# A decoder layer's state space tables padded on GpSimd, and its first h made in three steps

## The chip, the cores and the metric

The kernel runs on one NeuronCore of a Trainium2 chip. The metric is the device time of one launch in microseconds (us), taken as the median of several runs. TensorE is called PE in the views of the profile, its weight loads PEld, VectorE DVE, ScalarE ACT, GpSimd POOL, and SP is the engine whose queue issues the DMAs.

## The reference

One layer of a decoder over 256 tokens of width 2048, in float32:

```
mod = silu(c) @ w_ada + b_ada                      # six rows of 2048: sh1, sc1, g1, sh2, sc2, g2
h = rms_norm(x, norm1_g) * (1 + sc1) + sh1
q, k, v, u = split(h @ w_in)                       # 2048 -> 4 x 1024
attn = dilated_attention(rms_norm(q), rms_norm(k), v)   # 8 heads
y = gelu(s5_mixer(u))                              # 64 groups of 16 channels, 64 complex states each
ssm = y * sigmoid(y @ w_glu + b_glu)
x = x + g1 * (concat(rms_norm(attn), rms_norm(ssm)) @ w_out)
h2 = rms_norm(x, norm2_g) * (1 + sc2) + sh2
out = x + g2 * (square(relu(h2 @ w_ff1)) @ w_ff2)
```

The s5_mixer is a linear recurrence with a diagonal complex transition a per group: the state takes a times itself plus B u, and y = Re(C state) + D u.

## The kernel before

**Products.** Every large product is made from a high and a low part: a value v is written as hi, which is v rounded to the type that PE multiplies in one pass (fp32r), and lo = v - hi. Of the four products three are made (line 191, mm3). `split` (line 172) makes the parts of a tile: ScalarE copies v into hi with the rounding, VectorE subtracts. The same is done to each weight piece of 512 KB as it arrives in the ring `raw` of nine buffers (load_w, line 181); its parts are called wh and wl, with three buffers each.

**First h.** x lies transposed in the tile XT, 16 chunks of 128 channels by 256 tokens. rbc is the reciprocal root mean square per token, broadcast over partitions; g1c is (1 + sc1) * norm1_g per channel. make_h(kg) makes four chunks of h in the tiles HA or HB, both parts. Each chunk goes through a VectorE multiplication with rbc in place, a ScalarE pass in place that scales by g1c and adds the shift (line 316), a ScalarE copy that rounds to the high part, and a VectorE subtraction. make_h is called four times, with weight blocks of w_in between the calls.

**Modulation.** The product with w_ada (100 MB) is cut into 96 pieces. Eight of 24 blocks go through PE (line 249, then 260), the others through VectorE, which multiplies a piece of 128x1024 with c and sums it up (line 158). `pump` puts pieces between the other work in program order.

**State space tables.** B times powers of a is built by VectorE in b_step (tiles WB2, WB3), C times powers of a in ca_step (tile CA). Two groups share the 128 partitions, 64 each, and PE needs them block diagonal. So tables full of zeros are laid out by GpSimd memsets, and pad_write copies the lower 64 partitions into one set of columns and the upper 64 into another: two copies of 64 partitions. It fills padB (tile PD, four copies of 512 elements), the two padC (tiles WB0 and WB1, filled twice by toep_half, eight copies of 256 and eight of 768 elements), and wpad (tile PD, filled by four calls of wb_block, eight copies of 256 elements in each). toep_half's products give the tile TO (ScalarE evicts them in 32-partition pieces); wb_block's 16 transposes per call (line 504) give the final WB tiles, which are used much later, when u is complete. All of these copies are made on ScalarE (line 161, through the helper copy).

**Order.** The program is written once in order; a scheduler that simulates it by a model of the engines then decides the order of the instructions of each engine, and puts in the semaphores. Each engine works its own list in order. `issue_after` puts the cbc multiplications and the b_steps behind the end of the first make_h. Behind the first block of w_in come toep_half(0), a second block, toep_half(1), further blocks, make_h(1), and the wb_blocks.

Of the kernel before, what the change touches and what calls it, by code (L numbers as in the profile page):

```python
# [9 lines left out]
F32 = mybir.dt.float32  # L10
F32R = mybir.dt.float32r
I32 = mybir.dt.int32
AF = mybir.ActivationFunctionType
ALU = mybir.AluOpType
# [102 lines left out]
class _K:  # L117
# [5 lines left out]
    def t(self, tag, shape, dt=F32, bufs=1):  # L123
        self.n += 1
        return self.sb.tile(list(shape), dt, name=f"{tag}_{self.n}", tag=tag, bufs=bufs)
# [12 lines left out]
    def mul(self, out, a, b, eng=None):  # L138
        return self.tt(out, a, b, ALU.mult, eng)
# [14 lines left out]
    def stt(self, out, a, s, b, op0, op1, accum=None):  # L154
        if accum is None:
            self.nc.vector.scalar_tensor_tensor(out, a, s, b, op0=op0, op1=op1)  # L156
        else:
            self.nc.vector.scalar_tensor_tensor(out, a, s, b, op0=op0, op1=op1, accum_out=accum)  # L158

    def copy(self, out, a, scale=1.0):  # L160
        self.nc.scalar.activation(out, a, AF.Copy, scale=scale)  # L161

# [35 lines left out]
def _body(nc, tc, I, out, sb, ps):  # L198
    k = _K(nc, tc, I, out, (sb, ps))
    t, tr = k.t, k.tr  # L200
    mul, add, sub, ts, stt, copy = k.mul, k.add, k.sub, k.ts, k.stt, k.copy
# [5 lines left out]
    xTf = t("XT", [P, 16, SEQ])  # L207
# [20 lines left out]
    mod = t("mod", [P, 96])  # L228
# [12 lines left out]
    def ada_pieces(b):  # L241
        c4 = slice(4 * b, 4 * b + 4)
        if b in PE_BLOCKS:
            acc = tr()
            for g in range(4):
# [8 lines left out]
                if g < 3:  # L254
                    yield
            rows = t("rows", [P, NB], bufs=2)
            copy(rows, acc)
            pc = tr()
            for j in range(4):
# [34 lines left out]
    for j in range(16):  # L294
        sq = t("rows", [P, NB], bufs=2)[:, 0:SEQ]
        nc.scalar.activation(sq, xTf[:, j], AF.Square)
        q = 32 * (j % 4)
        mm(pss[q : q + 32, 0:SEQ], onek, sq, start=j < 4, stop=j >= 12)
    copy(rw[:, 1], pss[:, 0:SEQ])
    mm(psb[:, 0:SEQ], sel, rw[:, 1], start=True, stop=True)  # L300
    rbc = t("rbc", [P, SEQ])
# [3 lines left out]
    g1c = t("g1c", [P, 16])  # L305

    hs = {}

    def make_h(kg):
        hs[kg] = t("HA" if kg % 2 == 0 else "HB", [P, 2, 4, SEQ], F32R)  # L310
        c4 = slice(4 * kg, 4 * kg + 4)
        stt(g1c[:, c4], mod[:, 16 + 4 * kg : 20 + 4 * kg], 1.0, col["n1g"][:, c4], ALU.add, ALU.mult)
        for kc in range(4 * kg, 4 * kg + 4):
            v = xTf[:, kc]
            mul(v, v, rbc)
            nc.scalar.activation(v, v, AF.Identity, bias=mod[:, kc : kc + 1], scale=g1c[:, kc : kc + 1])
            end = k.split(hs[kg][:, 0, kc % 4], hs[kg][:, 1, kc % 4], v)
        return end.ins

    accs = {}  # L320
# [11 lines left out]
    def w_in_evict(pp, n):  # L332
        c = "uqkv"[n // 2]
        fresh = (c, n % 2) not in accs
        accs[c, n % 2] = True
        if c not in accs:
            if c in "uv":
                accs[c] = t(c.upper(), [P, 2, AW])
            else:
                if "qk" not in accs:  # L340
                    accs["qk"] = t("QK", [P, 2, 2, AW])
                accs[c] = accs["qk"][:, "qk".index(c)]
        for m in range(2):
            d = accs[c][:, m, NB * (n % 2) : NB * (n % 2) + NB]
            if fresh:
                copy(d, pp[m])
            else:
                add(d, pp[m], d)
# [120 lines left out]
    def pad_write(dst, src):  # L469
        for gp in range(2):  # L470
            pr = slice(64 * gp, 64 * gp + 64)
            copy(dst(gp)[pr], src[pr])


    padB = t("PD", [P, 32, 2, 2, 16])
# [16 lines left out]
    def wb_block(i):  # L492
        if i == 0:
            s5["wpad"] = t("PD", [P, 8, 2, 4, 2, 16])
            nc.gpsimd.memset(s5["wpad"], 0.0)
        wpad, w, rr = s5["wpad"], i // 2, slice(8 * (i % 2), 8 * (i % 2) + 8)
        for b in range(4):
            pad_write(lambda gp: wpad[:, :, :, b, gp, :], by_r(bpow[w][:, 3 - SUB[b], :, rr]))
        wb.append(t(f"WB{i}", [P, 8, 2, P]))
        for r in range(0, 8, 2):  # L500
            pt = tr()
            for e in range(4):
                src = wpad[:, r + e // 2, e % 2].rearrange("p s g j -> p (s g j)")
                nc.tensor.transpose(pt[:, P * e : P * e + P], src, ident)
            copy(wb[i][:, r : r + 2].rearrange("p r i n -> p (r i n)"), pt)
# [9 lines left out]
    def toep_half(h):  # L515
        for i, padC in enumerate(padCs):
            r8 = 16 * h + 8 * i
            pad_write(lambda gp: padC[:, :, :, gp, 0, :], by_r(c0[:, :, r8 : r8 + 8]))
            pad_write(
                lambda gp: padC[:, :, :, gp, 1:, :].rearrange("p r i d j -> p (r i) (d j)"),  # L520
                ca[:, r8 : r8 + 8, :, 0:3, :].rearrange("p r i d j -> p (r i) (d j)"),
            )
        pt = tr()
        pv = pt.rearrange("p (i g d j) -> p i g d j", i=4, g=2, d=4)
        for i in range(4):
            for ri in range(2):
                for q in range(4):
                    r = 4 * i + q
                    mm(
                        pv[32 * q : 32 * q + 32, i], padB[:, 16 * h + r, ri].rearrange("p g j -> p (g j)"),  # L530
                        padCs[r // 8][:, r % 8, ri].rearrange("p g d j -> p (g d j)"),
                        start=i == 0 and ri == 0, stop=False,
                    )
        mm(
            pv[:, :, :, 0, :], ident, dskip[:, 4 * h : 4 * h + 4].rearrange("p r (g j) -> p r g j", g=2),
            start=False, stop=True,
        )
        pq = pt.rearrange("p (i g d) -> p i g d", i=4, g=2)
        for q in range(4):
            for b in range(4):  # L540
                o = 16 * SUB[b]
                tq = toep[32 * b : 32 * b + 32, 16 * h + q : 16 * h + q + 13 : 4].rearrange("p r g s j -> p r g (s j)")
                copy(tq[:, :, :, o:], pq[32 * q : 32 * q + 32, :, :, 0 : 64 - o])
# [47 lines left out]
    s5_small()  # L591
    pump(8)
    h_end = make_h(0)
    ring["tags"] = RINGS[0]
    with tc.issue_after(rbc_end):
# [20 lines left out]
    for n in (6, 7):  # L616
        run(w_in_block(n, [0]), 1)
    make_h(1)
    ring["tags"] = RINGS[1]
    cw = t("T0", [P, 2, 2, 16, 16])  # L620
# [10 lines left out]
    ring["tags"] = RINGS[2]  # L631
    run(w_in_pair(4, [0, 1]), 3)
    make_h(2)
    run(w_in_block(0, [1, 2]), 4)
    run(w_in_block(1, [1, 2]), 4)
# [29 lines left out]
    for j in range(2):  # L665
        for m in range(2):
            v = qk[:, j, m].rearrange("p (h e) -> p h e", h=NH)
# [337 lines left out]
```

## Time and profile before

| | us |
|---|---|
| median of 3 runs | 1260.02 (1258.0 to 1260.76) |
| profiled execution, own time | 1261.61 |
| its span | 1259.8 |
| mean granted PE clock | 0.96 of full |

The span is the time from the first to the last recorded instruction. Busy time is summed by engine; an engine can be busy for a small share of the span and still hold up the others in one stretch, so the rows below are mostly taken by stretches. An idle time is shown with what ended it.

### The profile page before, as it was taken

The page shows a single profiled execution, that of the slowest core. Times are in us where ns is not written, and L with a number is a line of the kernel's source. Part 1 is how long each engine was busy: PE and PEld are TensorE (multiplying, and loading weights), DVE is VectorE, ACT ScalarE, POOL GpSimd, SP SyncE. Part 2 cuts the span into 40 slices and gives each one's busy share as a digit, 9 for nine tenths or more (in the row PEclk, how much of TensorE's full clock was granted, in tenths as well). Part 3 has the DMA queues.
Part 4 walks back from the last instruction along what each step waited for, and adds up shares of the span by engine and source line. Part 5 has one row for each costly group of instructions (what it writes and reads, how often), then busy time and mean ns, then how long its engine had stood idle before and what let it go on. Part 6 is the DMA issues. An engine that isn't in the chain of part 4 may idle for free.

```text
span 1259.8 us, 17899 instructions
## 1 busy us (share of the span) xinstructions
PE 1182.8 (94%) x6818; PEld 985.8 (78%) x6818; DVE 920.6 (73%) x1520; ACT 579.2 (46%) x808; POOL 13.0 (1%) x12
## 2 busy tenths in 40 slices
PE   5779999999988879399999999999999999999998
PEld 1457677866787768388888888888888888888887
DVE  9898679999687998867664567655667666768654
ACT  3789534333475334335444444443344443344432
POOL 3000000000000000000000000000000000000000
PEclk9689999999797989699999999999999999999999
DMA  9898999799574878656666666656667666777760
GB/s 365 308 313 298 357 333 325 259 320 335 212 239 131 289 235 278 232 183 213 219 187 186 212 233 226 214 186 193 221 221 252 190 189 186 236 237 236 227 209 26
DMA packets 82165, 299.58 MB, mean 238 GB/s; under 512 B 9120, under 2 KB 11424, under 8 KB 80288
## 3 DMA queue, kind: packets, MB, share of 16 engines
q1 hardware_dynamic: 82080, 298.45, 70.7%
q8 instruction: 53, 0.87, 0.3%
q14 instruction: 32, 0.26, 0.1%
HBM read 296.31 MB, written 2.10 MB: 237 GB/s over the span
## 4 chain that ended last, share of the span: by engine, by line
PE 76%; DVE 10%; DMA 7%; ACT 5%; issue 2%; DVEq 0%; ACTq 0%
PE acc L848 37%; PE acc L850 19%; DMA raw<-w_ada 6%; PE acc L193 3%; PE acc L194 3%; PE acc L195 3%; DVE wl L136 3%; DVE raw L158 2%; PE tr L249 2%; PE tr L848 1%; PE tr L553 1%; ACT wh L161 1%; ACT WB L161 1%; PE acc L690 1%; DVE XT L156 1%
## 5 line engine op out<-in xcount | busy, mean ns | idle before, releaser
L136 DVE TENSOR_TENSOR wl<-raw,wh 128x1024 fp32r<-128x1024 f32 x360 | 439.8, 1222 | 254.3 <-ACT wh L161 252.0
L161 ACT ACTIVATE wh<-raw 128x1024 fp32r<-128x1024 f32 x360 | 380.9, 1059 | 491.7 <-PE acc L848 336.6
L848 PE MATMUL acc<-CA,wh 128*128 128x512 f32 x608 | 167.8, 397 | 3.6 <-DVE rs L136 3.6
L158 DVE SCALAR_TENSOR_TENSOR raw<-raw,cbc 128x1024 f32<-128x1024 f32 x112 | 136.3, 1220 | 37.7 <-DMA raw<-w_ada 37.0
L848 PE MATMUL acc<-TO,wh 128*128 128x512 f32 x480 | 132.7, 398 | 1.6 <-DVE rows L136 1.6
L848 PEld LDWEIGHTS acc<-CA,wh 128*128 128x128 f32 x608 | 104.1, 188 | 17.7 <-issue 4.1
L848 PE MATMUL acc<-QK,wh 128*128 128x512 f32 x384 | 106.9, 399 | 7.0 <-DVE QK L136 6.9
L850 PEld LDWEIGHTS acc<-CA,wl 128*128 128x128 f32 x608 | 92.4, 188 | 13.5 <-DVE wl L136 0.3
L850 PE MATMUL acc<-CA,wl 128*128 128x256 f32 x608 | 96.2, 281 | 0.0
L848 PEld LDWEIGHTS acc<-TO,wh 128*128 128x128 f32 x480 | 83.0, 189 | 13.0 <-issue 1.8
L850 PEld LDWEIGHTS acc<-TO,wl 128*128 128x128 f32 x480 | 73.2, 188 | 10.6
L848 PEld LDWEIGHTS acc<-QK,wh 128*128 128x128 f32 x384 | 66.4, 190 | 15.9 <-issue 7.4
L850 PE MATMUL acc<-TO,wl 128*128 128x256 f32 x480 | 76.0, 280 | 0.0
L848 PE MATMUL acc<-WB,wh 128*128 128x512 f32 x256 | 69.8, 394 | 0.0
L850 PEld LDWEIGHTS acc<-QK,wl 128*128 128x128 f32 x384 | 58.5, 188 | 7.9
L850 PE MATMUL acc<-QK,wl 128*128 128x256 f32 x384 | 60.3, 279 | 0.0
L193 PE MATMUL acc<-wh,HA 128*128 128x512 f32 x128 | 47.8, 406 | 5.0 <-ACT wh L161 5.0
L194 PE MATMUL acc<-wl,HA 128*128 128x512 f32 x128 | 51.7, 404 | 0.0
L195 PE MATMUL acc<-wh,HA 128*128 128x512 f32 x128 | 50.5, 399 | 0.0
L194 PE MATMUL acc<-wl,HB 128*128 128x512 f32 x128 | 50.2, 396 | 0.2 <-DVE wl L136 0.2
L195 PE MATMUL acc<-wh,HB 128*128 128x512 f32 x128 | 49.2, 395 | 0.0
L193 PE MATMUL acc<-wh,HB 128*128 128x512 f32 x128 | 48.0, 399 | 0.5 <-DVE V L136 0.4
(269 smaller groups left out, 1739.1 us busy)
## 6 DMA issues: line engine op xcount, KB each, us to landing
raw<-w_ff SPq DMA_DIRECT2D x256, 512.0 KB, 4.4
raw<-w_ada SPq DMA_DIRECT2D x158, 512.0 KB, 5.3
raw<-w_in SPq DMA_DIRECT2D x64, 512.0 KB, 6.5
raw<-w_out SPq DMA_DIRECT2D x32, 512.0 KB, 4.9
U<-w_ada SPq DMA_DIRECT2D x8, 1024.0 KB, 7.6
XT<-xT SPq DMA_DIRECT2D x8, 512.0 KB, 5.8
T<-w_ada SPq DMA_DIRECT2D x8, 512.0 KB, 6.6
raw<-w_glu SPq DMA_DIRECT2D x8, 512.0 KB, 8.0
```

The costliest lines, as they stand in the source:

```text
L136: return (eng or self.nc.vector).tensor_tensor(out, a, b, op=op)
L156: self.nc.vector.scalar_tensor_tensor(out, a, s, b, op0=op0, op1=op1)
L158: self.nc.vector.scalar_tensor_tensor(out, a, s, b, op0=op0, op1=op1, accum_out=accum)
L161: self.nc.scalar.activation(out, a, AF.Copy, scale=scale)
L193: mm(ps, xh, wh, start=start, stop=False)
L194: mm(ps, xh, wl, start=False, stop=False)
L195: mm(ps, xl, wh, start=False, stop=stop)
L249: mm(acc[32 * q : 32 * q + 32, :], cpad[:, 4 * g + q, :], raw[:, i, :], start=g == 0, stop=g == 3,)
L553: mm(pv[:, r - r2, ri], wb[r // 8][:, r % 8, ri], u2[:, :, r, :], start=True, stop=True)
L690: mm(pv[pr, r - r8], ca[pr, r, ri].rearrange("p s j -> p (s j)"), H[pr, ri, r, :], start=False, stop=ri == 1,)
L848: mm(pp[e], hi[:, e, kk], xs[kk].rearrange("p s n -> p (s n)"), start=first and kk == 0, stop=False)
L850: mm(pp[e][:, 0:SEQ], lo[:, e, kk], xs[kk][:, 0], start=False, stop=last and kk == 3)
```

## The change

pad_write copies on GpSimd in place of ScalarE. make_h takes three steps for each chunk in place of four: VectorE multiplies x by g1c and by rbc in one instruction, ScalarE adds the shift and writes the rounded high part in one pass, and VectorE adds the shift again and subtracts the high part for the low part. The helper stt_i is stt with the instruction returned.

```
+    def stt_i(self, out, a, s, b, op0, op1):
+        return self.nc.vector.scalar_tensor_tensor(out, a, s, b, op0=op0, op1=op1)
...
         for kc in range(4 * kg, 4 * kg + 4):
-            v = xTf[:, kc]
-            mul(v, v, rbc)
-            nc.scalar.activation(v, v, AF.Identity, bias=mod[:, kc : kc + 1], scale=g1c[:, kc : kc + 1])
-            end = k.split(hs[kg][:, 0, kc % 4], hs[kg][:, 1, kc % 4], v)
+            v, hi, lo, sh = xTf[:, kc], hs[kg][:, 0, kc % 4], hs[kg][:, 1, kc % 4], mod[:, kc : kc + 1]
+            stt(v, v, g1c[:, kc : kc + 1], rbc, ALU.mult, ALU.mult)
+            nc.scalar.activation(hi, v, AF.Identity, bias=sh)
+            end = k.stt_i(lo, v, sh, hi.bitcast(F32), ALU.add, ALU.subtract)
         return end.ins
...
         for gp in range(2):
             pr = slice(64 * gp, 64 * gp + 64)
-            copy(dst(gp)[pr], src[pr])
+            nc.gpsimd.tensor_copy(dst(gp)[pr], src[pr])
```

## Rows read from the trace of the kernel before

**Rows 1.** Page: busy us of each engine, share of the span, instructions.

```profile
PE 1182.8 (94%) x6818; PEld 985.8 (78%) x6818; DVE 920.6 (73%) x1520; ACT 579.2 (46%) x808; POOL 13.0 (1%) x12
```

**Rows 2.** Busy time by stretch; last three: granted PE clock, DMA share, GB/s.

```profile
28.00:56.00 28.00, 18.11 (x132) 9.06 (x133) 22.78 (x43) 17.69 (x29) 0.00 (x0) 0.63 0.88 325
56.00:72.00 16.00, 12.23 (x53) 7.16 (x52) 13.43 (x25) 15.61 (x31) 0.00 (x0) 0.98 0.83 286
72.00:90.00 18.00, 17.39 (x122) 13.70 (x120) 18.00 (x34) 12.39 (x25) 1.82 (x1) 0.83 0.93 320
90.00:126.00 36.00, 31.19 (x161) 24.56 (x162) 31.82 (x60) 35.01 (x69) 0.00 (x0) 1.00 0.90 304
126.00:220.00 94.00, 93.56 (x411) 70.90 (x410) 71.55 (x102) 42.89 (x54) 0.22 (x1) 1.00 0.92 338
```

**Rows 3.** Waits in 26:56, 56:82 and 82:126: total us, times, longest.

```profile
DVE HA L136 <- ACT HA L161: 5.0, 2, 3.5
...
PE acc L193 <- ACT wh L161: 3.8, 1, 3.8
...
PE tr L504 <- ACT PD L161: 4.0, 4, 1.5
...
DVE wl L136 <- ACT wh L161: 4.2, 4, 1.4
```

**Rows 4.** Timeline of VectorE, ScalarE and PE, 28 to 90: start, us, instruction.

```profile
28.16 1.43 DVE L136 TENSOR_TENSOR XT<-XT,rbc 128x256 f32<-128x256 f32 x4
...
47.89 3.42 ACT L161 ACTIVATE WB<-CA 64x768 f32<-64x768 f32 x4 [4.44 <-DVE CA L136]
48.91 0.15 DVE L136 TENSOR_TENSOR mod<-tr,small 128x4 f32<-128x4 f32 x1
51.33 2.07 ACT L316 ACTIVATE XT<-XT,mod,g1c 128x256 f32<-128x256 f32 x4
...
55.48 0.48 PE L193 MATMUL acc<-wh,HA 128*128 128x512 f32 x1
...
70.13 1.06 ACT L161 ACTIVATE wh<-raw 128x1024 fp32r<-128x1024 f32 x1
```

**Rows 5.** ScalarE by form, 25 to 127: busy us, mean ns | idle before.

```profile
L161 ACT ACTIVATE PD<-WB 64x256 f32<-64x256 f32 x32 | 13.3, 417 | 0.7
L161 ACT ACTIVATE WB<-CA 64x768 f32<-64x768 f32 x8 | 6.7, 843 | 4.6 <-DVE CA L136 4.4
L161 ACT ACTIVATE WB<-T 64x256 f32<-64x256 f32 x8 | 3.3, 411 | 5.8 <-DVE T L150 5.8
L161 ACT ACTIVATE PD<-WB 64x512 f32<-64x512 f32 x4 | 2.5, 629 | 4.8 <-DVE WB L136 4.8
L161 ACT ACTIVATE HA<-XT 128x256 fp32r<-128x256 f32 x4 | 1.5, 406 | 0.0
```

**Rows 6.** VectorE and ScalarE by form, whole span, as in rows 5.

```profile
L136 DVE TENSOR_TENSOR XT<-XT,rbc 128x256 f32<-128x256 f32 x16 | 5.6, 419 | 0.0
L156 DVE SCALAR_TENSOR_TENSOR V<-XT,g2c,rbc 128x256 f32<-128x256 f32 x8 | 3.3, 481 | 0.0
L136 DVE TENSOR_TENSOR wl<-raw,wh 128x1024 fp32r<-128x1024 f32 x360 | 439.8, 1222 | 254.3 <-ACT wh L161 252.0
L907 ACT ACTIVATE TO<-V,mod 128x256 fp32r<-128x256 f32 x8 | 3.3, 495 | 3.3 <-DVE V L156 3.3
```

**Rows 7.** Timeline of GpSimd and VectorE, at the start and near 81 us.

```profile
2.47 3.58 POOL L480 MEMSET WB<- 128x2048 f32 x2
4.34 1.74 DVE L152 TENSOR_SCALAR HA<-HA 128x32 f32<-128x32 f32 x1
14.77 0.17 DVE L152 TENSOR_SCALAR HA<-HA 128x32 f32<-128x32 f32 x1
...
80.76 1.82 POOL L495 MEMSET PD<- 128x2048 f32 x1 [69.17 <-PE tr L529]
81.30 0.15 DVE L136 TENSOR_TENSOR adap<-adap 128x1 f32<-128x1 f32 x1
```

## The prediction

> **What bounds the kernel now.** I began with the busy shares of the page: TensorE (PE) is busy 94% of the span, ScalarE (ACT) 46% [rows 1]. Over the whole kernel ScalarE bounds nothing, so a relief of ScalarE can only count in a stretch where its queue is the last to deliver. The second view was therefore the busy time by stretch [rows 2]. The reader is to see three things there. From 28 to 126 us PE is idle for 28 - 18.11, 16 - 12.23, 18 - 17.39 and 36 - 31.19, together 19.1 us; from 126 to 220 us it is idle for 0.4 us in 94. ScalarE is busy 15.61 of 16 us and 35.01 of 36 us in two of those stretches, and 42.89 of 94 behind them. And VectorE (DVE) is nearly full in the same stretches: its idle time there is 5.2 + 2.6 + 0 + 4.2 = 12.0 us. All that the diff edits, but for the later uses of make_h, runs before 126 us. So the question is how far PE's full stretch can start before 126 us; what it gains there should reach the end, since PE stays full behind it.
>
> The third view was the waits [rows 3]: PE waits 3.8 us at one place for the high part of a weight tile (wh) from ScalarE, 4.0 us for the padded table PD, VectorE 4.2 us for wh, and 5.0 us for the high part of the first h (HA). The fourth was the sequence on ScalarE around the first h [rows 4], the fifth the groups of copies on it [rows 5].
>
> **The change part by part.** *Copies that leave ScalarE.* pad_write issues 32 copies of 64x256 and 4 of 64x512 into PD, and 8 of 64x256 and 8 of 64x768 into the WB tiles: 13.3 + 2.5 + 3.3 + 6.7 = 25.8 us of ScalarE [rows 5]. On the path they count in three places.
>
> (a) Before the first h. The shift of h is added to mod at 48.91, done at 49.06, but ScalarE is in four 64x768 copies from 47.89 and starts the first L316 pass at 51.33 [rows 4]: 2.3 us. The four L316 passes then run (2.07 us) before the first HA copy (0.41 us [rows 5]), so the high part of chunk 0 is done at 53.8; in the new order one pass writes it, about 0.5 us after its start (a pass of the same form, L907, takes 495 ns [rows 6]). That would be 49.6, 4 us earlier. But PE takes the 64 table matmuls of toep_half(0) in front of the first L193, which starts at 55.48 [rows 4], and these need the four 64x768 copies. So the gain is between 0 (the copies on GpSimd end where they end now) and 4; I take 2.5, since the multiplications moved off VectorE (below) also let those copies begin earlier.
>
> (b) The second input block. PE waits 3.8 us for wh [rows 3], which ScalarE starts at 70.13 [rows 4] after copies and evictions without a gap. Two 64x256 and two 64x768 copies, 2.5 us, and two HA copies, 0.8 us, are among them after 56 us. The wait can go whole; what is late next is VectorE, which has 2.6 us idle in this stretch. Gain between 0 and 3.8; I take 2.5.
>
> (c) The four wb_block calls, which begin behind the memset of PD at 80.76 [rows 7]. 32 copies, 13.3 us, leave a ScalarE that is 97% busy from 90 to 126. PE's waits there are 4.0 for PD and VectorE's 4.2 for wh [rows 3]. The wait for PD isn't removed but moved: PE's transposes now wait for GpSimd. Gain between 0 and 5; I take 1.
>
> *Copies that arrive at GpSimd.* It is idle but for memsets. The trace has no copy on it. Its 128x2048 memset takes 1.8 us [rows 7], 0.88 ns an element, so an estimate for 256 elements from below is 0.23 us; from above I take ScalarE's 0.417 for the same copy, doubled, 0.83. I take 0.4, next to ScalarE's row. If nothing holds it up, GpSimd does a wb_block's 8 copies in 3.3 us, as ScalarE does now.
>
> *What GpSimd does to VectorE.* At 4.34 a 128x32 TENSOR_SCALAR takes 1.74 us, to the end of a memset; the same operation takes 0.17 at 14.77, when GpSimd is quiet. At 81.30, in the middle of a memset, a two-input TENSOR_TENSOR takes 0.15 us [rows 7]. So a memset shuts out one class of VectorE instruction and not the other, and no row shows a GpSimd instruction that reads. The cost of 52 copies to VectorE lies between nothing and their whole length. VectorE has gaps for those of (a) and (b) but hardly for the 32 of (c): between 0 and 32 x 0.417 = 13.3, less its 4.2 us idle, so 9.1. I take 2, near the lower end, because the row for two-input instructions shows no hold.
>
> The page "SBUF — State Buffer" of the Trainium skill (section "Who interferes with whom") speaks against that choice: a VectorE instruction with two SBUF inputs does contend with a GpSimd instruction that reads SBUF, not with one that only writes, and the later of the two blocks until the first is through. The memset row agrees with the second half; the first half is not shown here. By it the cost would be the upper end, which is the first rival below.
>
> *The first h.* ScalarE loses 16 copies of 128x256 (406 ns [rows 5]), four to a make_h, with their place in the chain; 16 L316 passes become passes that write the high part. VectorE keeps two instructions per chunk: TENSOR_TENSOR 419 ns becomes SCALAR_TENSOR_TENSOR 481 ns, twice, so 32 x 0.06 = 1.9 us in all [rows 6]; before 126 us there are two make_h, 1 us. The moved part matters more: the 16 multiplications by rbc run early today, from 28.16 on [rows 4]; in the new form they need g1c. Twelve leave this stretch, 12 x 0.35 us (5.6 us busy over 16) = 4.2 us, so the ca steps that feed the first tables can end as much earlier; four return with the second make_h, 1.4 us into a full VectorE, the rest behind 126 us, where VectorE has 22 us idle up to 220 [rows 2]. Net cost 1 us; bounds 0 and 2.4. No DMA, semaphore queue of SP or loop order is edited. But the order on each engine is made by a scheduler that simulates the program, so a few places may come out in another order: an estimate of 2 us either way, of the size of the single waits in rows 3.
>
> *Sum:* -2.5 - 2.5 - 1 + 2 + 1 = -3, and -2 more for what starts earlier behind it: VectorE's 5.0 us wait for HA [rows 3] goes in part, and the b_steps, which the code puts behind the first h, come as much earlier. That is -5. The profiled execution took 1261.61 (span 1259.8, 1.8 around it), which gives 1256.6. It lies 1.6 above the median of 1260.02, so I predict 1255.0.
>
> **The rivals.** *1, slower: GpSimd and VectorE shut each other out.* Place: the wb_blocks. Each 64x256 copy waits for the VectorE instruction under way (up to 1.22 us [rows 6]) and holds the next for 0.42: a wb_block needs up to 8 x 1.64 = 13.1 us where ScalarE needs 3.3. Four are 52 us, and from the memset of PD at 80.76 + 1.82 to 126 there are 43, so the last is 9 us late; VectorE's own sum gives 9.1 as well. PE takes its transposes in order and stands behind them. Less the 6 us of (a) and (b) it is +3: 1263; without that gain, 1269. It decides once a copy costs VectorE or the queue over some 0.3 us each. For it: VectorE is full there, and the held TENSOR_SCALAR. Against: the unhindered two-input row. *2, no change: the early gain finds no data.* DMA is busy 83 to 93% of these stretches [rows 2], so its idle time from 28 to 126 is 3.4 + 2.7 + 1.3 + 3.6 = 11 us, and VectorE has 12. If buffers come free no sooner, one or two us are left: 1259. For it: DMA and VectorE are as full as ScalarE over the whole of 28 to 126. Against: the DMA share is lowest just where ScalarE was full, 56 to 72 us. *3, more: all the waits go,* 4 + 3.8 + 5 - 1 = 11.8, about as much as DMA's and VectorE's idle time allow: 1248.
>
> **How the numbers follow.** Forecast, 1252 to 1257.5: 0.38. Rival 3: 0.12. Rival 2: 0.22. Rival 1: 0.28. A difference under 0.2% (2.5 us) can't be told from none here. So faster 0.50, same 0.22, slower 0.28. The range 1246 to 1269 takes in rival 3 with the order's 2 us and rival 1 to its upper end; the likeliest case alone is 1251 to 1258.
>
> **What would show it.** Right: the first L193 at 51 to 54 us, no wait of PE for wh near 70, ScalarE under 75% from 90 to 126, PE full from about 121. Wrong: two-input VectorE instructions of 128x1024 well over 1.22 us next to GpSimd copies, PE waiting for GpSimd's PD in front of L504, or PE full from 126 as now. It fails if GpSimd's copies are over 0.8 us each.

## The result, and the profile after

The changed kernel takes 1273.36 us (median of 4 runs, 1272.53 to 1273.73) against 1260.39 (1258.0 to 1261.63) beside it: a ratio of 1.0104, interval 1.0087 to 1.0122, so 13 us slower [11.0, 15.4]. The prediction said 1255.0, in a range of 1246 to 1269. The median and all four runs are outside it.

The page of the changed kernel, its line of busy times, answers to [rows 1]:

```profile
PE 1187.1 (93%) x6818; PEld 987.0 (78%) x6818; DVE 929.6 (73%) x1520; ACT 549.1 (43%) x740; POOL 63.3 (5%) x64
```

ScalarE is relieved of 30 us as foreseen. VectorE, with as many instructions as before, is busy 9.0 us longer. The busy time by stretch, columns as in [rows 2], shows where the full stretch of PE was lost:

```profile
28.00:56.00 28.00, 18.25 (x81) 8.22 (x82) 27.41 (x38) 9.66 (x14) 12.32 (x12) 0.76 0.84 325
56.00:72.00 16.00, 14.25 (x144) 9.29 (x142) 7.27 (x11) 11.63 (x24) 6.77 (x8) 1.00 0.85 294
72.00:90.00 18.00, 14.26 (x89) 10.93 (x82) 18.00 (x34) 11.38 (x23) 7.19 (x7) 0.91 0.91 316
90.00:126.00 36.00, 29.01 (x131) 23.01 (x129) 36.00 (x62) 18.87 (x27) 16.70 (x16) 0.91 0.90 317
126.00:220.00 94.00, 86.67 (x387) 67.60 (x388) 72.21 (x113) 36.52 (x46) 9.35 (x11) 0.95 0.88 320
```

Two readings. From 90 to 126 ScalarE fell from 35.01 of 36 us to 18.87, VectorE rose from 31.82 to 36.00, and PE lost 2.2 us: VectorE, with no idle time left, took over as the bound. And from 126 to 220, where PE had been idle for 0.4 us, it is now idle for 7.3. The prediction had said that PE "stays full behind it". The waits of PE in 28 to 130 and, below the dots, in 195 to 260 (total us, times, longest) say on what:

```profile
PE acc L197 <- DVE wl L136: 11.1, 3, 5.0
PE acc L196 <- ACT HA L319: 5.3, 1, 5.3
...
PE acc L196 <- ACT HB L319: 5.4, 1, 5.4
```

wl waits are VectorE's; the last row is the h of input stage 3, for which PE waits until 210.8 us, over 60 us behind the last of the copies. The timeline of VectorE, ScalarE and PE (start, us, instruction) has the first h and that later one:

```profile
47.90 0.80 PE L196 MATMUL acc<-wh,HA 128*128 128x512 f32 x1 [5.29 <-ACT HA L319]
48.92 3.36 DVE L161 SCALAR_TENSOR_TENSOR HA<-XT,mod,HA 128x256 fp32r<-128x256 f32 x4
...
210.02 0.16 DVE L136 TENSOR_TENSOR mod<-adap,small 128x4 f32<-128x4 f32 x1
210.21 1.71 ACT L319 ACTIVATE HB<-XT,mod 128x256 fp32r<-128x256 f32 x4 [3.77 <-DVE mod L136]
```

The first input matmul starts at 47.90 instead of 55.48 [rows 4], 7.6 us earlier. By the count of the 768 input matmuls that both traces have (h times w_in, lines 193 to 195 before), all of it is gone by the 384th (180.7 us, 180.6 before); the 480th is 2.0 us late, the 528th, behind the wait for HB, 9.6, and the 768th 11.6. The low part of h takes 840 ns a piece at 48.92, beside 64x768 copies on GpSimd; such an instruction took 481 [rows 6]. Last, GpSimd's copies by form (busy us, mean ns, idle before):

```profile
L475 POOL COPY PD<-WB 64x256 f32<-64x256 f32 x32 | 31.2, 975 | 31.8 <-PE tr L507 12.5 <-DVE WB L136 8.7 <-DVE adap L136 6.9
L475 POOL COPY WB<-CA 64x768 f32<-64x768 f32 x8 | 10.5, 1307 | 10.5 <-DVE CA L136 10.1
L475 POOL COPY WB<-T 64x256 f32<-64x256 f32 x8 | 3.8, 472 | 24.8 <-DVE T L150 16.8 <-PE tr L532 7.7
```

The same 64x256 copy takes 472 ns into the WB tables and 975 into PD, most of them beside a full VectorE; ScalarE did both in 0.41 [rows 5].

### The profile page after: what moved, and what is told of

The parts are those of the page before. It is cut to its first block, busy times and chain, and to the rows that moved or that the text cites. A ratio compares the mean times of both kernels' runs of the same rounds, so it can differ in the third digit from the quotient of the medians.

```text
span 1271.7 us, 17901 instructions
## 1 busy us (share of the span) xinstructions
PE 1187.1 (93%) x6818; PEld 987.0 (78%) x6818; DVE 929.6 (73%) x1520; ACT 549.1 (43%) x740; POOL 63.3 (5%) x64
## 4 chain that ended last, share of the span: by engine, by line
PE 76%; DVE 13%; DMA 6%; issue 2%; ACT 2%; SPq 0%; DVEq 0%
PE acc L851 38%; PE acc L853 19%; DMA raw<-w_ada 5%; DVE raw L158 3%; PE acc L196 3%; PE acc L197 3%; PE acc L198 3%; DVE wl L136 3%; PE tr L252 2%; PE tr L851 1%; PE tr L556 1%; DVE XT L156 1%; DVE V L136 1%; DMA PD<-w_ada 1%; ACT wh L164 1%
## 5 line engine op out<-in xcount | busy, mean ns | idle before, releaser
L851 PEld LDWEIGHTS acc<-QK,wh 128*128 128x128 f32 x384 | 66.3, 190 | 15.4 <-issue 5.2
L196 PE MATMUL acc<-wh,HA 128*128 128x512 f32 x128 | 49.6, 422 | 7.0 <-ACT HA L319 5.3
L198 PE MATMUL acc<-wh,HA 128*128 128x512 f32 x128 | 52.7, 416 | 0.0
```

What stands on the lines that cost most here:

```text
L196: mm(ps, xh, wh, start=start, stop=False)
L198: mm(ps, xl, wh, start=False, stop=stop)
L851: mm(pp[e], hi[:, e, kk], xs[kk].rearrange("p s n -> p (s n)"), start=first and kk == 0, stop=False)
```

## The experiments

Differences are given in us of 1260, from the ratio to the kernel before, run beside each, with its interval. The runs are called e1 to e19 in the order in which they stand here; no run has the number 6. Theories: **A**, the wb_block copies are slow on GpSimd, so that PD and what is loaded over it come late. **B**, the copies hold VectorE (the prediction's first rival). **C**, the multiplications moved behind the scale carry it.

**Each part alone.** Three-step make_h with the copies on ScalarE (`copy` kept in pad_write):

> The three-step h alone; all padded copies stay on ScalarE. Theory A (the wb_block copies are slow on GpSimd, PD and T0 come free late, the DMAs of the modulation pieces behind them wait, and make_h(3) waits for its shift): the loss is not in this kernel, so it keeps part of the earlier start of the first h, 1255 to 1259, that is 0 to 5 us under before. Theory B (GpSimd holds VectorE, in proportion to copy time): the same, 1256 to 1260. Theory C (the multiplications by rbc, now behind g1c, and the order they bring cost the time): 1268 to 1273.

Measured: +14.5 [11.3, 17.6]. Only the copies, four-step make_h kept:

```
-            copy(dst(gp)[pr], src[pr])
+            nc.gpsimd.tensor_copy(dst(gp)[pr], src[pr])
```

> All padded copies on GpSimd, make_h in four steps as before. Theory A and B: the whole loss is here, 1270 to 1276 (before 1260). Theory C: 1258 to 1262. In the trace, by A, the first DMA into PD for a modulation piece is issued some 30 us later than before (before 123.9) and the DMA share from 126 to 160 us falls from 0.96 to about 0.72.

Measured: +18.0 [15.0, 21.2]. The changed kernel with the 32 wb_block copies back on ScalarE, then with those of padB and padCs back:

```
+            if eng == "act":
+                copy(dst(gp)[pr], src[pr])
```

> The changed kernel with the 32 copies of the four wb_block calls back on ScalarE; the 20 copies into padB and the padCs stay on GpSimd. Theory A: the late release of PD goes, 1254 to 1259. Theory B: 19 of 50 us of GpSimd copy time stay, so about two fifths of the loss: 1263 to 1266. Theory C: 1270 to 1273.

> The changed kernel with the 20 copies into padB and the padCs back on ScalarE; the 32 wb_block copies on GpSimd. Theory A: the loss stays, 1270 to 1276, with PD still free about 30 us late. Theory B: three fifths of the loss, 1266 to 1269. Theory C: 1270 to 1273.

Measured: +6.3 [3.8, 8.8] and +8.3 [5.7, 10.7]. Either half alone costs more than both together, and taking back either group of copies helps by 5 to 7 us: no sum of fixed prices for A, B and C does that. A fourth theory, **D**: each edit makes the scheduler come to another order of issue, and the stalls of that order are the loss. At 810 of the 6261 places in PE's list of matmuls, the changed kernel has one of other tiles or another shape than the kernel before.

**One suspect at a time.** For A, no modulation piece is loaded over T0 or PD (`RINGS[2] = ('raw',)`) in the changed kernel. For B, the kernel before with 32 extra GpSimd copies of the same table pieces into a tile that nobody reads. For C, the four steps with the multiplication moved behind the scale:

```
+                nc.gpsimd.tensor_copy(scr[pr].rearrange("p (r i j) -> p r i j", r=8, i=2), src[pr])
...
-            mul(v, v, rbc)
-            nc.scalar.activation(v, v, AF.Identity, bias=mod[:, kc : kc + 1], scale=g1c[:, kc : kc + 1])
+            stt(v, v, g1c[:, kc : kc + 1], rbc, ALU.mult, ALU.mult)
+            nc.scalar.activation(v, v, AF.Identity, bias=mod[:, kc : kc + 1])
```

For D, the kernel before with its first pump at 2.25 instead of 2.5: the same instructions, and 354 of PE's places filled otherwise.

> The changed kernel in which the modulation pieces behind make_h(1) no longer use the tiles T0 and PD as buffers, only the ring raw. Theory A (PD and T0 come free 20 to 30 us later, and that starves the DMA queue): the loss from 126 us on goes, 1260 to 1266, and the DMA share from 126 to 160 us is back above 0.85. Theory B or D: 1268 to 1278.

> The kernel before, its padded copies on ScalarE as they are, and besides 32 copies on GpSimd of the same 64x256 table pieces into a scratch tile that nobody reads; the order of the instructions on TensorE, VectorE, ScalarE and SP stays as before but for some ten places each. So it adds the hold of VectorE by GpSimd and nothing else. Theory B (the hold is the loss): two-input VectorE instructions beside a copy take 0.2 to 0.4 us longer, 7 to 11 us in all, and the time rises by 5 to 9 to 1266 to 1270. Theory D (each edit gives the scheduler another order on the engines, and the stalls of that order are the loss): the hold is there in the trace, but the time rises by 0 to 3, 1260 to 1264.

> The kernel before with make_h still in four steps, but with x multiplied by g1c and rbc in one VectorE instruction (so behind g1c) and the scale taken out of the ScalarE pass: no instruction is saved or added on any engine, only the place of 16 multiplications moves. Theory D: this alone changes the order and costs most of what the three-step h cost, 1267 to 1276. If the three-step h lost by something else (ScalarE's pass or the low part's instruction): 1259 to 1263.

> The kernel before with one number of the interleaving changed (2.25 in place of 2.5 pieces of modulation work behind each piece of the first blocks of w_in): the same instructions, another order. Theory D: up to 1265 to 1272. If the order makes little difference, as theories A to C have it: 1259 to 1262.

Measured: +10.1 [6.9, 13.2] without the loads over PD; +2.1 [-0.1, 4.5] with the extra copies, whose order was that of before but for a dozen places; +16.5 [13.9, 19.0] with the late multiplication; +15.8 [12.0, 19.4] with nothing but the pump. The last is the surprise: no instruction is added, removed or moved to another engine, and the time is over what D gave, as it is with the late multiplication. A is a small part at most. Its sign is there: in e2 the first load into PD is issued at 153.0 us and not at 123.9, and the DMA share from 126 to 160 us is 0.78 and not 0.96. But PE is busy in 34.00 of those 34 us.

**Other orders of the changed kernel.** First pump at 2.25 and 2.75, the fourth at 1.75, and e3 with the fourth at 1.75:

```
-PUMPS = (2.5, 2.75, 1.0, 1.5, 0.75, ...
+PUMPS = (2.25, 2.75, 1.0, 1.5, 0.75, ...
```

> The changed kernel with its first pump at 2.25 instead of 2.5: the same instructions on the same engines, issued in another order. Theory D (the loss of the changed kernel is in the order that its scheduler came to, not in its copies): the time moves by 5 to 15 us either way from 1273, to anywhere between 1258 and 1285. Theories A and B (slow table copies on GpSimd, or VectorE held beside them): 1270 to 1276, since every copy is still there.

> The changed kernel with its first pump at 2.75: as the run with 2.25. Theory D: not the same time as at 2.5 or 2.25, spread of over 5 us among the three; theories A and B: 1270 to 1276 again.

> The changed kernel with the pump of the output block's stretch (the fourth) at 1.75 instead of 1.5. Theory D: moves by over 5 us in one direction; if one of the three orders is without the waits for h of stage 3 that the trace of the changed kernel shows between matmuls 480 and 624, it comes to 1258 to 1263. Theories A and B: 1270 to 1276.

> The changed kernel with the 32 copies into wb_block on ScalarE (as in e3, 1266.9) and the fourth pump at 1.75. Theory D: another order, 5 us or more from e3's time on either side, 1256 to 1275. Theory A (e3 gained because the wide table is ready early): stays at 1265 to 1269.

Measured: +22.6, +23.6, +10.5 and +4.2 [1.9, 6.4]. Half of what D said: two orders move the changed kernel by some 10 us; the other two move it by 2 to 3, from 13 and from 6, which their intervals don't tell from nothing; and none comes to under the kernel before. The fourth (e13) misses D's numbers and meets A's. In none of these runs could the edits be told from the order.

**The edits in the order of before.** These do tell them apart. The kernel builds the program of before, reads from it the order on each engine, and then ties every instruction that both have to its neighbour of that order on its engine (an ordering edge without a wait; the code is shortened):

```
for key in order:                       # of the kernel before
    x = by.get(key)                     # the same instruction here
    if x is None or key[0] in FREE:     # FREE: left to the scheduler
        continue
    e = str(x.engine)
    if e in last: tc.add_manual_dep(x, last[e].name, NoSync)
    last[e] = x
```

FREE holds the first multiplications in the runs with the three-step h, these and the copies in the fourth run, and nothing in the others. With no edit this gives the order of before exactly. The first three runs have the order of before; the fourth has the instructions of before in the order of the changed kernel.

> The whole change, with the order of the kernel before: every instruction that both kernels have is chained to its neighbour of the kernel before on its engine, so that PE, SP, ScalarE and VectorE issue in that order; the copies run on GpSimd, the 16 first multiplications stand where the scheduler puts them. Theory D (the loss is the new order): the 13 us go, 1252 to 1263, and with what the prediction's steps are worth without an order (-5) about 1256. Theories A and B (the copies on GpSimd are slow and hold VectorE): 1268 to 1276 again, for every copy is still on GpSimd. Theory C (the moved multiplications): over 1268 as well.

> The table copies on GpSimd and the four-step h (as e2, which took 1279), in the order of the kernel before on PE, VectorE, ScalarE and SP. Theory D: 1257 to 1264, 15 us less than e2. Theories A and B: 1272 to 1280, as e2.

> The three-step h and the copies on ScalarE (as e1, which took 1274), in the order of the kernel before but for the 16 first multiplications. Theory D: 1256 to 1263. Theory C: 1270 to 1275, as e1.

> The reverse: the instructions of the kernel before (copies on ScalarE, four-step h), held in the order that the changed kernel's scheduler came to; copies and first multiplications stand where the scheduler puts them. Theory D: slow without any part of the change, 1268 to 1285. Theories A, B, C: 1258 to 1264, as the kernel before, since nothing that they blame is in it.

Measured: the whole change +3.0 [1.1, 4.9]; the copies alone +6.6 [4.9, 8.3]; the three-step h alone -1.8 [-3.2, -0.4]; none of the change, but its order, +17.1 [15.4, 19.0]. D holds for the larger part: in its new order the kernel is slow without any edit, and in the old one the edits cost 3 where they cost 13. Run by run, the order that the scheduler came to costs 10.1 us more than the old one for the whole change, 11.4 for the copies alone (18.0 less 6.6) and 16.3 for the three-step h alone (14.5 and -1.8). But the whole change (1264.1) is just over D's range, and the copies alone (1268.7) lie between D's and that of A and B: the copies have a price of their own, more than e7 gave. The waits of PE in 195 to 260 in the kernel with the instructions of before and the new order:

```profile
PE acc L200 <- ACT HB L168: 6.4, 1, 6.4
```

It is the wait for stage 3's h that the changed kernel shows (5.4), and the kernel before and the whole change in the old order don't. By the count of input matmuls this kernel is 3.9 us late at the 192nd, 6.4 at the 480th and 13.8 at the 528th. From the 480th to the 528th it and the changed kernel lose 7.4 and 7.6 us, so nearly half of the 17 us of the order has its place there.

**Which copies.** In the order of before, first the three-step h with only the 20 copies of padB and padCs on GpSimd; then the four-step h with only the 32 of the wb_blocks (`wide` marks these, WB_TOO says which group goes to GpSimd):

```
-            (nc.gpsimd.tensor_copy if PADS[0] else copy)(dst(gp)[pr], src[pr])
+            (nc.gpsimd.tensor_copy if PADS[0] and WB_TOO == wide else copy)(dst(gp)[pr], src[pr])
```

> Three-step h and the 20 copies of toep_half on GpSimd, the 32 of the wb_blocks on ScalarE, in the order of the kernel before. If the wb_block copies carry the 6.6 us: 1254 to 1260, at or under the three-step h alone (ratio 0.9986). If the toep_half copies do: 1262 to 1267.

> The 32 copies of the wb_blocks on GpSimd, those of toep_half on ScalarE, four-step h, in the order of the kernel before. If the wb_block copies carry the 6.6 us: 1265 to 1270. If they cost only what the 32 extra copies of e7 cost beside the old ones (ratio 1.0017): 1261 to 1264.

Measured: -6.2 [-8.8, -3.5] for e18 and +5.8 [3.5, 8.1] for e19. The wb_block copies carry the price, the others pay; e18 beats both kernels: 1256.31 us (median of 7 runs, 1250.07 to 1257.91) against 1260.99 beside it. The medians are 4.7 us apart, the ratio gives 6.2. Busy time by stretch of e18, columns as in [rows 2]:

```profile
28.00:56.00 28.00, 18.91 (x120) 6.70 (x121) 27.83 (x36) 7.64 (x12) 14.38 (x17) 0.65 0.89 341
56.00:72.00 16.00, 15.92 (x106) 10.16 (x105) 15.20 (x26) 12.58 (x24) 3.58 (x4) 1.00 0.76 252
72.00:90.00 18.00, 14.44 (x90) 10.56 (x88) 18.00 (x37) 16.02 (x33) 1.82 (x1) 1.00 0.99 385
90.00:126.00 36.00, 33.63 (x168) 27.27 (x168) 35.23 (x64) 31.88 (x60) 0.00 (x0) 1.00 0.92 327
126.00:220.00 94.00, 93.56 (x411) 70.94 (x410) 75.21 (x109) 38.53 (x44) 0.22 (x1) 1.00 0.92 339
```

PE gains 3.7 us from 56 to 72, loses 3.0 from 72 to 90, where VectorE is full in both kernels, gains 2.4 from 90 to 126, and is full behind that as before. VectorE fills up from 28 to 56 (27.83 us, 22.78 before). The same of e19, its VectorE groups from 90 to 132, and the tiny ones (128x1) among them by duration (ns: shortest, median, longest):

```profile
90.00:126.00 36.00, 27.44 (x141) 21.54 (x142) 36.00 (x60) 21.07 (x35) 24.77 (x25) 1.00 0.83 282
126.00:220.00 94.00, 93.56 (x409) 71.25 (x408) 68.89 (x98) 42.88 (x57) 0.22 (x1) 0.98 0.91 330
...
L158 DVE SCALAR_TENSOR_TENSOR raw<-raw,cbc 128x1024 f32<-128x1024 f32 x13 | 16.8, 1304 | 0.0
L136 DVE TENSOR_TENSOR wl<-raw,wh 128x1024 fp32r<-128x1024 f32 x11 | 14.3, 1304 | 1.7 <-ACT wh L168 1.7
L136 DVE TENSOR_TENSOR T<-CA,sm 128x512 f32<-128x512 f32 x4 | 3.0, 778 | 0.0
...
L136 DVE TENSOR_TENSOR adap<-adap x8: 148/340/349, 91.8 to 128.2; 128x1 f32<-128x1 f32 x8
```

PE loses 3.7 us from 90 to 126 and nothing up to 220. By the count of input matmuls e19 is level with the kernel before at the 48th, 4.6 us late at the 192nd (133.1 us) and still 4.6 at the 768th (299.1 us). The other 4.3 us by which its span is longer come behind that, where nothing is edited, and are not explained; the profiled execution, 1270.60 us, was the slowest of six (median 1266.69). ScalarE is 14 us lighter from 90 to 126 and it helps no one: VectorE is full, and each of its two-input groups is longer on average (1218 and 1221 ns before for the first two, 684 for the third; the tiny ones took 147 to 155). PE's waits from 90 to 132, of before and, in the second fence, of e19:

```profile
PE tr L504 <- ACT PD L161: 4.0, 4, 1.5
PE acc L193 <- ACT wh L161: 1.2, 2, 1.0
PE acc L194 <- DVE wl L136: 0.2, 1, 0.2
```

```profile
PE tr L525 <- POOL PD L492: 4.4, 3, 2.3
PE acc L201 <- DVE wl L136: 4.2, 4, 1.3
```

So it is VectorE's lateness with wl, 4.0 us more, that PE pays for; its wait for PD stays what it was, on another engine. How VectorE and GpSimd hold each other is to be seen in the timeline of GpSimd and VectorE of e19:

```profile
97.40 1.41 DVE L158 SCALAR_TENSOR_TENSOR raw<-raw,cbc 128x1024 f32<-128x1024 f32 x1
97.79 4.02 POOL L492 COPY PD<-WB 64x256 f32<-64x256 f32 x3
98.74 0.34 DVE L136 TENSOR_TENSOR adap<-adap 128x1 f32<-128x1 f32 x1
...
103.50 0.15 DVE L136 TENSOR_TENSOR adap<-adap 128x1 f32<-128x1 f32 x1
103.57 1.21 DVE L158 SCALAR_TENSOR_TENSOR raw<-raw,cbc 128x1024 f32<-128x1024 f32 x1
```

Beside the copies this 128x1024 instruction takes 1.41 us and the tiny one 0.34; between two groups of copies they take 1.21 and 0.15. Single instructions are either unhindered or about 0.20 us longer, whatever their length: from 90 to 132 the 128x1024 ones take 1.21 to 1.23 or 1.41 to 1.42. Each side waits for the other: the three copies take 1.28 to 1.34 us each. Over the whole stretch from 28 us on, VectorE's busy time is 901.44 us in e19 against 895.37 of before: 6.1 us for 32 copies, 0.19 each.

## Why the prediction was wrong

The failed step is the order on the engines. The prediction named the scheduler ("a few places may come out in another order"), left it out of the sum and bounded it by "an estimate of 2 us either way, of the size of the single waits". The runs show +10 here (the change in its own order, 13, less in the old one, 3) and +17 for that order without the change. A single wait is the wrong yardstick: 810 places are not a few, and the loss is a string of waits. The longest, for HB at 210 us, lies where "PE stays full" was taken as given. Why HB and the others come late in this order wasn't traced further. Every kernel that was run in a new order of its own was slower than the kernel before, by 4 to 24 us, whatever was in it, so here the order was no coin with two sides. Whether a better order than that of before exists for these instructions stays open.

A second term was mis-sized, and the old order shows it alone. *(c) and the hold of VectorE:* -1 and +2, together +1. Measured, +5.8 for the wb_block copies alone, and 9.2 as the difference of the whole change in the old order (e14) and e18 (3.0 and -6.2; 7.7 by medians). That is the first rival's place and mechanism, and its point of decision was met: a 64x256 copy takes 0.97 us on average and not 0.4, over the 0.8 at which the prediction said that it fails. That its price (9.1) comes out too is partly luck: it had 1.64 us for a copy and up to 13.3 us for VectorE, and e19 shows 0.99 and 6.1. The choice near the lower end rested on [rows 7], a two-input instruction unhindered by a memset. A memset reads nothing, so that row had no say on copies. The sentence of the Trainium skill that spoke against the choice ("SBUF — State Buffer", section "Who interferes with whom") is borne out by the trace: two SBUF inputs beside a GpSimd instruction that reads, 0.34 us for 0.15 and 1.41 for 1.21. The hold isn't the whole copy, as the upper end assumed, but 0.19 us of VectorE for each; what made it dear is that VectorE had no idle time left to absorb it. The 32 extra copies of e7, beside those on ScalarE, hold VectorE nearly as much (5.3 us more busy) and cost only 2.1 [-0.1, 4.5]; there PE's PD still came from ScalarE, its wait for it from 90 to 132 fell to 2.2 us, and for wl it was 3.2. In e19 the two are 4.4 and 4.2, together 3.2 more. By the count of input matmuls e7 is 1.6 us late at the 192nd and e19 4.6, 3.0 more. So of these 3 us some 2 are PE's wait for PD, late from a GpSimd that itself waits for VectorE, and 1 its wait for wl.

The rest stood in its sum. *(a), (b), the multiplications and what follows* were -2.5, -2.5, +1 and -2: -6. (The first rival calls this "the 6 us of (a) and (b)", which alone are 5.) The run that has just these, in the old order, gives -6.2, or -4.7 by medians; e18 is 6.1 us ahead at the 192nd input matmul. That the sum fits so closely is luck, for the split is another one: the first input matmul of e18 starts at 55.6, no earlier than before, since PE waits 6.5 us there for the WB tables from GpSimd, as the lower bound of (a) had it; by the 48th input matmul it is 6.4 us ahead, and the 3.8 us wait for wh [rows 3] is gone. In the changed kernel's own order (a) came out at 7.6 and was lost again.

So the account runs: -6.2 for the h and the toep_half copies, +9.2 for the wb_block copies, +10.1 for the order, 13.1 in all. It holds for this sequence of differences; taken the other way round, the order costs 17.1 without the edits, and the edits then give 4 back. By the prediction's own terms, with (c) and hold at 9 and the order at 0, it would have been 1263, its first rival; the whole change in the old order takes 1264.1.

Of what it named as signs: no wait for wh near 70 us was half right (1.7 left), ScalarE under 75% from 90 to 126 right (52%), the first matmul earlier than named, and PE full from about 121 us wrong. Two-input instructions "well over 1.22 us" (from 25 to 127 us the 17 for wl take 1.28 on average) and the copies over 0.8 us were both seen; PE waiting for GpSimd's PD was not, in this kernel, but is in e19.

## What to carry to other kernels

Before an engine is relieved, look at the idle time of the one that will be last next: the same kind of copy paid where VectorE had gaps (28 to 72 us) and cost where it was full. When a scheduler sets the order, any edit is also a change of order, and that can outweigh the edit; hold the order fixed and try the edit in it, or change the order alone, before judging either. A row bounds an unknown cost only if it has what causes the cost, here a read.

## What the runs showed of the hardware

A copy on GpSimd with VectorE idle takes as long as on ScalarE (0.41 and 0.84 us [rows 5]): 0.40 us for 64x256, 0.83 for 64x768. From 59 to 67 us of the changed kernel (ns: shortest, median, longest):

```profile
L475 POOL COPY WB<-T x4: 394/398/402, 59.3 to 63.4; 64x256 f32<-64x256 f32 x4
L475 POOL COPY WB<-CA x4: 827/1266/1819, 60.2 to 65.6; 64x768 f32<-64x768 f32 x4
```

Beside two-input VectorE instructions that run back to back, a 64x256 copy takes about as long as the instruction that it waits for: up to 1.4 us in e19. The VectorE instruction that it holds takes 0.20 us longer, half of the copy's own 0.40, at every length seen (0.15 to 0.34, 1.21 to 1.41). Beside 64x768 copies the hold is about 0.56 us: of the four low parts of h at 48.92 us of the changed kernel, three take 1.04 us and one 0.47.

One and the same program can spread over 12 us: the four runs of the changed kernel with the fourth pump at 1.75 took 1263.2, 1268.1, 1273.6 and 1274.9 us, at a mean granted TensorE clock of 0.969, 0.964, 0.956 and 0.957. The order of the times is nearly that of the clocks, while before's 13 runs beside them spread over 4 us (1260.28 to 1264.35). It isn't so everywhere: of the ten runs of e7 (1258.56 to 1267.35) the one at a clock of 0.913 took 1266.23. What the clock followed wasn't tried.
